# Order of the sparse-attention projections and index scores in a two-layer hybrid trunk

## The chip, the cores and the metric

One core of a Trainium2 chip runs the whole program in one launch. The metric is device time in microseconds (us): the median of repeated executions. TensorE is called PE here, VectorE DVE, ScalarE ACT, GpSimd POOL, SyncE SP, as in the profile's rows. L12 is line 12 of the kernel.

## The reference, cut to what matters

Two layers, 512 tokens of width 1024, float32. Each layer normalizes x and feeds one combined projection `w_in` into four branches: a gated convolution, a sparse attention with an indexer, a gated linear recurrence, and a cross-attention into 256 memory tokens. Each branch is lifted to width 1024, multiplied by its own sigmoid gate and summed; then an output projection with a residual, and a gated FFN with a residual.

The sparse attention is the part that the change touches. For each block of 128 queries:

```
rel    = relu(einsum('thd,sd->ths', iq, ik) * 64**-0.5)   # 8 index heads
score  = einsum('ths,th->ts', rel, iw);  future keys -> -inf
sel    = top 128 keys of score
p      = softmax(q @ k[sel] * 64**-0.5);  out = p @ v[sel]
```

The columns of `w_in` that feed it lie side by side: 512 for the queries, then 64 for the keys, 64 for the values and 512 + 64 + 8 for the index queries, the index keys and the index weights.

## The kernel before

Every big product is done as three matmuls of 32-bit parts: an operand is split into a high and a low part (hi, lo), and `mm3` (L318 to L328) adds hi*hi, hi*lo and lo*hi in PSUM (L324, L325, L327). Activations are kept split (`h_hi`, `h_lo`). A weight chunk (`Chunk`, L228) is loaded in parts of at most 1024 columns per partition by SP's DMA queue into `w_raw` (4 buffers); ACT copies the part to `w_hi` (L100) and DVE subtracts to get `w_lo` (L257), three buffers each, both at high priority. PE can use the part only after that. A chunk of 256 columns over all 1024 rows has two parts, one of 456 columns has four.

PSUM tiles come from three rotating groups: `mm` (3 banks), `at` (2) and `tr` (3).

A layer's mixer first runs four generators that each do a step and yield (L1033 to L1039). The order of their steps is a string of letters, `EARLY` (L45), one string for each layer:

- `b` is `projections` (L1008), three steps. Step one: the chunk of 256 columns (keys, values and the first two index heads), four token blocks of 24 matmuls each, evicted by `key_out` and worked up by `key_heads` (norm, rotation, transposes). Step two: the chunk of 456 columns (six index heads, the index key, the index weights), 96 matmuls for the four token blocks into three `mm` banks and one `tr` bank, evicted by `index_out`, worked up by `index_heads`. Step three: the queries, two chunks of 256 columns, 192 matmuls, then `query_heads`.
- `m` is `mem_branch` (L747), ten steps: a projection of two memory heads (48 matmuls of 512 columns), four steps of attention into the memory tokens (12 matmuls of 256 columns and four transposes each), and both once more.
- `c` is `conv_branch` (L715), six steps of 48 matmuls of 512 columns each.
- `s` is the selection: `select(1)`, `select(2)`, `select(3)` (L985) one after the other, five yields each. The first step of each is the scoring: for each of eight heads two matmuls ("dots", L841 and L842) into an `at` bank, a Relu on ACT into a scratch tile, and a multiply-add on DVE into `score` (L994, L996). `score` has one buffer, so a selection's scoring on DVE starts only when the one before is done. Four more steps hold four rounds each of MAX8 (L1002) and MATCH_REPLACE8 (L1003) on DVE, sixteen rounds in all, and a last operation writes the mask `bias` (L1006).
- `n` is the late norm, in the second layer only.

The scratch tile of the scoring is `wide()`, a group of four buffers, which `key_out`, `index_out` and the queries also use. Another group, `scratch512` (tile name `sq`, two buffers), holds squares of the norms and of the memory projection.

When the string is used up, `lift(3)` runs with six selection steps after each of its four steps (`weave`, L1039). Then `values` and `lift(0)` run woven with the attention blocks `attend(0)` to `attend(3)` (L844). An attention block needs `dots` of queries with keys, a masked maximum on DVE (L857), Exp on ACT, a reciprocal on DVE (L860), a scaling on ACT, and transposes of the probabilities on PE (L871). `attend(0)` needs no selection: its mask is the causal one. The first gate projection of `lift(0)` does its hi*hi and lo*hi products for all weights first and its products with `w_lo` at the end.

The letters and weaves give only a program order. A planner orders each engine's instructions when the program is built: it takes, on its own estimates of durations, the ready instruction of the highest priority, where earlier in the program means higher, and the weight splits and PSUM evictions are lifted above the rest. On the chip each engine then runs its list in that fixed order.

`after_two` and `after_los` (L226, L264 to L270) hold back named instructions until the next chunk's splits have been issued.

Of the kernel before, what the change touches and what calls it, by code (L numbers as in the profile page):

```python
# [25 lines left out]
KD = D // P  # L26
# [15 lines left out]
NONC = -2.0e38  # L42
OFF = -1.0e30
AHEAD = 3000
EARLY = ["mmbmcmcbmmmscsmcsssmccmbs", "mnmbmcmcbmmmscsmcsssmccmbs"]  # L45
MM_BUFS = 3
TR_BUFS = 3
AT_BUFS = 2
# [23 lines left out]
def hybrid_trunk(ctx: ExitStack, tc: tile.TileContext, x, mem, positions, norm_mix, w_in, conv_w,  # L72
# [33 lines left out]
    def mm_ps():  # L106
        return pmm.tile([P, 512], F32, name="mm")
# [4 lines left out]
    def tr_ps():  # L112
        return pat.tile([P, 512], F32, name="tr", bufs=TR_BUFS)
# [32 lines left out]
    ps = tr_ps()  # L146
# [16 lines left out]
    ps = tr_ps()  # L163
# [64 lines left out]
    class Chunk:  # L228
        def __init__(self, src, kt, n):
            self.kt, self.step = kt, min(kt, 1024 // n)  # L230
            self.parts = []
            for k in range(0, kt, self.step):
                e = min(kt, k + self.step)
                m = (e - k) * n
                raw, hi, lo = (wpool.tile([P, 1024], dt, name=nm, bufs=b)[:, :m].rearrange("p (k n) -> p k n", n=n)
                               for nm, dt, b in (("w_raw", F32, RAW_BUFS), ("w_hi", F32R, W_BUFS), ("w_lo", F32R, W_BUFS)))
                if len(src.shape) == 2:
                    loaded[0] = nc.sync.dma_start(raw, src[k * P:e * P].rearrange("(k p) n -> p k n", p=P))
                    raw_loads.append(loaded[0])
                    if len(raw_loads) == 2:  # L240
                        tc.add_manual_dep(mem_half.ins, loaded[0].ins.name, order, reason="weights first")
                    if keys:
                        tc.add_manual_dep(loaded[0].ins, keys.pop().ins.name, order, reason="keys first")
                else:
                    for g in range(2):
                        nc.sync.dma_start(raw.rearrange("p k (g c) -> p k g c", g=2)[:, :, g, :], src[:, k:e, g, :])
                with tc.high_priority(offset=AHEAD):
                    if len(raw_loads) == 1:
                        dve.tensor_copy(hi[:, 1:, :], raw[:, 1:, :])
                        i = A(hi[:, :1, :], raw[:, :1, :], AF.Copy)  # L250
                    else:
                        i = A(hi, raw, AF.Copy)
                    while len(self.parts) == 1 and before_second:
                        tc.add_manual_dep(i.ins, before_second.pop().ins.name, order, reason="probabilities first")
                    while behind:
                        tc.add_manual_dep(i.ins, behind.pop().ins.name, order, reason="accumulators first")
                    i2 = dve.tensor_sub(lo, raw, f(hi))  # L257
                    while low_after:
                        tc.add_manual_dep(low_after.pop().ins, i2.ins.name, order, reason="weights first")
                    while low_behind:  # L260
                        tc.add_manual_dep(i2.ins, low_behind.pop().ins.name, order, reason="operands first")
                    while after_hi:
                        tc.add_manual_dep(after_hi.pop().ins, i.ins.name, order, reason="weights first")
                    for a in after_two:  # L264
                        tc.add_manual_dep(a.ins, i.ins.name, order, reason="weights first")
                    for a in after_los:
                        tc.add_manual_dep(a.ins, i2.ins.name, order, reason="weights first")
                self.parts.append((range(k, e), hi, lo))
            after_two.clear()
            after_los.clear()  # L270
# [9 lines left out]
    def wchunk(src, kt, n):  # L280
        return Chunk(src, kt, n)
# [22 lines left out]
    def tokens_wide(ws, a, kt, pss, first=0, in_turn=False):  # L304

        k0, behind_part = 0, None
        for w in ws:
            for ks, _, _ in w.parts[0 if k0 else first:]:
                made = []
                for t, ps in enumerate(pss):  # L310
                    for k in ks:
                        made += mm3(ps, pair(a, k0 + k, slice(t * P, (t + 1) * P)), w.at(k), k0 + k == 0, k0 + k == kt - 1)
                for i in made if in_turn and behind_part is not None else []:
                    tc.add_manual_dep(i.ins, behind_part.ins.name, order, reason="part by part")
                behind_part = made[-1]
            k0 += w.kt
# [133 lines left out]
    h = new_h()  # L450
# [183 lines left out]
    def mixer(l, h, norms, cm):  # L634
# [197 lines left out]
        with pool_("dsa") as dp:  # L832
# [60 lines left out]
            with pool_("idx") as ip:  # L893
# [5 lines left out]
                def wide():  # L899
                    return ip.tile([P, S], F32, name="wide", bufs=4)  # L900
# [63 lines left out]
                def index_out(ps, t):  # L964
                    u = wide()
                    with tc.high_priority(offset=AHEAD):
                        A(u[:, :7 * HD], ps[:, :7 * HD], AF.Copy, scale=r_t[:, t:t + 1])
                        A(iw[:, t, :], ps[:, 7 * HD:7 * HD + 8], AF.Copy, scale=r8_t[:, t:t + 1])
                    return u

                def index_heads(u, t):
                    w = by_head(u)
                    rope(w[:, :7], 7, t)
                    dve.tensor_copy(w[:, 7, :], w[:, 6, :])
                    ps = turn_heads(u, 4)
                    twin_to(ikS, ps[:, 3 * P:], t)
                    heads_to(iqS, 2, ps[:, :3 * P], 6, t)
# [7 lines left out]
                def select(t):  # L985
                    n = (t + 1) * P
                    score = ip.tile([P, S], F32, name="score", bufs=1)[:, :n]
                    for hh in range(8):
                        ps = at_ps()[:, :n]
                        dots(ps, iqS, ikS, hh, t, n)  # L990
                        rel = wide()[:, :n]
                        A(rel, ps, AF.Relu, scale=HD ** -0.5)
                        if hh == 0:
                            dve.tensor_scalar(score, rel, iw[:, t, 0:1], 0.0, op0=OP.mult, op1=OP.add)  # L994
                        else:
                            dve.scalar_tensor_tensor(score, rel, iw[:, t, hh:hh + 1], score, op0=OP.mult,  # L996
                                                     op1=OP.add)
                    dve.copy_predicated(score[:, t * P:], future, neg.to_broadcast([P, P]))
                    yield
                    for i in range(TOPK // 8):  # L1000
                        m8 = ip.tile([P, 16], F32, name="m8", bufs=2)[:, :8]
                        dve.max(m8, score)  # L1002
                        dve.match_replace(score, m8, score, REPL)  # L1003
                        if i % 4 == 3:
                            yield
                    dve.tensor_scalar(biases[t], score, REPL, OFF, op0=OP.not_equal, op1=OP.mult)  # L1006

                def projections():  # L1008
                    w = wchunk(w_in[l][:, C_DK:C_DK + 256], KD, 256)
                    for t in range(NT):  # L1010
                        ps = mm_ps()[:, :256]
                        tokens(w, h, t, ps)
                        key_heads(key_out(ps, t), t)
                    yield
                    w = wchunk(w_in[l][:, C_DK + 256:C_DK + 712], KD, 456)
                    pss = [mm_ps()[:, :456] for _ in range(MM_BUFS)] + [tr_ps()[:, :456]]
                    tokens_wide([w], h, KD, pss, in_turn=True)
                    for t, u in enumerate([index_out(ps, t) for t, ps in enumerate(pss)]):
                        index_heads(u, t)
                    yield  # L1020
                    us = [wide() for _ in range(NT)]
                    for c in range(2):
                        w = wchunk(w_in[l][:, C_DQ + c * 256:C_DQ + (c + 1) * 256], KD, 256)
                        for t in range(NT):
                            ps = mm_ps()[:, :256]
                            tokens(w, h, t, ps)
                            with tc.high_priority(offset=AHEAD):
                                A(us[t][:, c * 256:(c + 1) * 256], ps, AF.Copy, scale=r_t[:, t:t + 1])
                            if c:
                                query_heads(us[t], t)  # L1030
                    yield
# [653 lines left out]
```

## Time and profile before

| quantity | value |
|---|---|
| median of 3 runs | 1975.92 us (1974.9 to 1976.09) |
| the profiled execution's own time | 1974.79 us |
| its span in the profile | 1972.8 us |
| mean granted TensorE clock | 0.998 of full speed |
| PE busy | 1958.9 us (99%) |
| DVE busy | 1466.6 us (74%) |
| ACT busy | 1169.3 us (59%) |

The span leaves out 1.99 us of the profiled execution that lie before and after the profile's first and last instruction. The profiled execution is 1.13 us below the median of the three runs. A "busy" PE includes waits that are hidden by the pipelined ends of matmuls, and a share of busy time is a mean over stages with different limits.

### The profile page before, as it was taken

To read this page: it belongs to the slowest core of one execution; us is meant where nothing else is said; L and a number is where in the kernel's file an instruction comes from. 1 tells how busy PE (TensorE), PEld (TensorE's weight loads), DVE (VectorE), ACT (ScalarE), POOL (GpSimd) and SP (SyncE) were. 2 spreads that over 40 slices of the span, in tenths; PEclk is the share of its full clock that TensorE was granted. 3 is DMA by queue.
4 is the path that set the end of the run, shared out by engine and by line. 5 is a ranking of instruction groups with operands and counts; after the bars stand their busy time and mean duration, and the time that the engine had idled before them with its cause. 6 is when DMAs were issued, how large, how long until landed. Compare 5 with 4: busy or idle time off the path is not lost.

```text
span 1972.8 us, 26656 instructions
## 1 busy us (share of the span) xinstructions
PE 1958.9 (99%) x9687; PEld 1636.0 (83%) x9687; DVE 1466.6 (74%) x2569; ACT 1169.3 (59%) x1958; POOL 236.2 (12%) x288
## 2 busy tenths in 40 slices
PE   9999999999999999999999999999999999999999
PEld 8888987878888888888888898878888888888887
DVE  7866998657876677786876699965678667867777
ACT  6754654766765456645654556477667655656564
POOL 1011111111111111100001111111111110111000
PEclk9999999999999999999999999999999999999999
DMA  8677666667687888886677767677777778898754
GB/s 304 207 179 168 172 160 166 161 139 172 166 210 186 231 232 255 244 245 188 202 218 168 181 144 174 148 182 157 167 177 162 209 198 251 250 266 235 213 186 139
DMA packets 222228, 385.25 MB, mean 195 GB/s; under 512 B 13194, under 2 KB 118224, under 8 KB 221840
## 3 DMA queue, kind: packets, MB, share of 16 engines
q1 hardware_dynamic: 163008, 244.16, 39.3%
q0 software_dynamic: 52192, 132.81, 33.3%
q10 hardware_dynamic: 6896, 6.58, 1.0%
q8 instruction: 76, 1.25, 0.3%
q14 instruction: 56, 0.46, 0.1%
HBM read 368.81 MB, written 140.51 MB: 258 GB/s over the span
## 4 chain that ended last, share of the span: by engine, by line
PE 97%; DVE 3%; ACT 0%; issue 0%; DVEq 0%; ACTq 0%
PE mm L327 24%; PE mm L324 23%; PE mm L325 23%; PE at L324 4%; PE at L325 4%; PE at L327 4%; PE tr L324 2%; PE tr L327 2%; PE tr L325 2%; PE tr L871 1%; PE tr L882 1%; PE tr L1577 1%; DVE score L1003 1%; PE at L842 1%; PE at L841 1%; DVE m L1002 1%
## 5 line engine op out<-in xcount | busy, mean ns | idle before, releaser
L100 ACT ACTIVATE w_hi<-w_raw 128x1024 fp32r<-128x1024 f32 (+1 forms) x435 | 457.3, 1054 | 353.1 <-PE mm L325 113.3
L324 PE MATMUL mm<-h_hi,w_hi 128*128 128x512 f32 x960 | 377.4, 394 | 0.6 <-DVE zg L1076 0.6
L325 PE MATMUL mm<-h_lo,w_hi 128*128 128x512 f32 x960 | 376.6, 392 | 0.0
L327 PE MATMUL mm<-h_hi,w_lo 128*128 128x512 f32 x960 | 374.8, 397 | 0.7 <-DVE w_lo L257 0.7
L1288 DVE TENSOR_TENSOR w_lo<-w_raw,w_hi 128x1024 fp32r<-128x1024 f32 x211 | 256.3, 1218 | 130.0 <-ACT w_hi L100 129.3
L257 DVE TENSOR_TENSOR w_lo<-w_raw,w_hi 128x1024 fp32r<-128x1024 f32 (+1 forms) x224 | 272.2, 1217 | 105.4 <-ACT w_hi L100 103.9
L1303 POOL DMA_DIRECT2D up_sums<-in_ffn_w_up_dram x120 | 121.5, 1012 | 836.5 <-DMA up_sums<-in_ffn_w_up_dram 554.6
L327 PEld LDWEIGHTS mm<-h_hi,w_lo 128*128 128x128 f32 x960 | 182.7, 190 | 37.6 <-DVE w_lo L257 0.8
L324 PEld LDWEIGHTS mm<-h_hi,w_hi 128*128 128x128 f32 x960 | 180.4, 188 | 36.3 <-issue 1.0
L325 PEld LDWEIGHTS mm<-h_lo,w_hi 128*128 128x128 f32 x960 | 180.4, 188 | 35.6 <-issue 0.2
L325 PE MATMUL mm<-w_lo,h_hi 128*128 128x512 f32 (+2 forms) x488 | 169.4, 347 | 0.3 <-DVE w_lo L257 0.3
L327 PE MATMUL mm<-w_hi,h_lo 128*128 128x512 f32 (+2 forms) x488 | 169.5, 347 | 0.0
L324 PE MATMUL mm<-w_hi,h_hi 128*128 128x512 f32 (+2 forms) x488 | 163.8, 347 | 0.0
L1303 POOL DMA_DIRECT2D w_sums<-in_ffn_w_down_dram x66 | 62.3, 944 | 331.8 <-DMA w_sums<-in_ffn_w_down_dram 186.2
L325 PEld LDWEIGHTS mm<-w_lo,h_hi 128*128 128x128 f32 x488 | 92.3, 189 | 11.3 <-DVE w_lo L257 0.6
L324 PEld LDWEIGHTS mm<-w_hi,h_hi 128*128 128x128 f32 x488 | 92.3, 189 | 10.5 <-ACT w_hi L100 0.2
L327 PEld LDWEIGHTS mm<-w_hi,h_lo 128*128 128x128 f32 x488 | 92.3, 189 | 10.2
L100 ACT ACTIVATE prob<-prob,small 128x128 f32<-128x128 f32 (+3 forms) x128 | 68.8, 554 | 33.6 <-DVE small L857 24.5
L327 PE MATMUL mm<-y_hi,w_lo 128*128 128x512 f32 x192 | 75.5, 393 | 0.0
L325 PE MATMUL mm<-y_lo,w_hi 128*128 128x512 f32 x192 | 75.4, 393 | 0.0
L324 PE MATMUL mm<-y_hi,w_hi 128*128 128x512 f32 x192 | 75.4, 393 | 0.0
L325 PE MATMUL mm<-w_lo,a_hi 128*128 128x512 f32 x160 | 63.2, 395 | 0.0
(496 smaller groups left out, 4191.6 us busy)
## 6 DMA issues: line engine op xcount, KB each, us to landing
w_raw<-in_w_in_dram SPq DMA_DIRECT2D x140, 512.0 KB, 4.6
up_sums<-in_ffn_w_up_dram POOLq DMA_DIRECT2D x120, 512.0 KB, 7.0
w_raw<-up_sums SPq DMA_DIRECT2D x80, 512.0 KB, 5.3
w_raw<-in_ffn_w_up_dram SPq DMA_DIRECT2D x60, 512.0 KB, 4.6
w_sums<-in_ffn_w_down_dram POOLq DMA_DIRECT2D x54, 512.0 KB, 6.1
up_sums<-up_sums POOLq DMA_DIRECT2D x40, 512.0 KB, 5.1
w_raw<-in_w_lift_dram SPq DMA_DIRECT2D x32, 512.0 KB, 4.6
w_raw<-in_ffn_w_down_dram SPq DMA_DIRECT2D x24, 512.0 KB, 5.0
```

Of the source, the lines that this page charges most:

```text
L100: i = act.activation(dst, src, func, **kw)
L257: i2 = dve.tensor_sub(lo, raw, f(hi))
L324: made += [pe.matmul(ps, ah, bh, start=first, stop=False, skip_group_check=more), pe.matmul(ps, ah, bl, start=False, stop=False, skip_grou ...
L325: pe.matmul(ps, ah, bl, start=False, stop=False, skip_group_check=more)]
L327: made += [pe.matmul(ps, al, bh, start=False, stop=last, skip_group_check=more)]
L841: return [pe.matmul(ps, q[:, hh, s], k[0][:, :n], start=True, stop=False), pe.matmul(ps, q[:, hh, s], k[1][:, :n], start=False, stop=True)]
L842: pe.matmul(ps, q[:, hh, s], k[1][:, :n], start=False, stop=True)]
L871: turn = pe.transpose(pp[:, (2 * e + i) * P:(2 * e + i + 1) * P], probs[2 * i + e][:, b * P:(b + 1) * P], ident)
L882: i = pe.matmul(pv[e * HD:(e + 1) * HD, c], vt[:, b, :], pt[:, b, e * 2 * P:(e + 1) * 2 * P], start=b == 0, stop=b == t)
L1002: dve.max(m8, score)
L1288: two = A(hi, raw, AF.Copy), dve.tensor_sub(lo, raw, f(hi))
L1303: i = nc.gpsimd.dma_start(dst, src, **kw)
```

## The change

The three steps of `projections` are put in another order: the chunk of 456 index columns first, then the chunk of 256 key columns, then the queries. The two `EARLY` strings are changed so that the index chunk stands behind one memory step (in the second layer behind the late norm too), the key chunk behind two more memory steps, the scoring of `select(1)` behind six memory steps and one convolution step in place of seven and two, and the scoring of `select(2)` ahead of the queries in place of behind them. Each letter occurs as often as before. The Relu of the scoring writes a `scratch512` tile in place of a `wide` tile. In `Chunk`, the instructions held in `after_two` and `after_los` wait for the first two parts of a chunk, not for all of them.

```diff
-EARLY = ["mmbmcmcbmmmscsmcsssmccmbs", "mnmbmcmcbmmmscsmcsssmccmbs"]
+EARLY = ["mbmmbcmmmsccsmmcsssmsccmb", "mnbmmbcmmmsccsmmcsssmsccmb"]
...
-                    for a in after_two:
+                    for a in after_two if len(self.parts) < 2 else []:
                         tc.add_manual_dep(a.ins, i.ins.name, order, reason="weights first")
-                    for a in after_los:
+                    for a in after_los if len(self.parts) < 2 else []:
                         tc.add_manual_dep(a.ins, i2.ins.name, order, reason="weights first")
...
                     for hh in range(8):
                         ps = at_ps()[:, :n]
                         dots(ps, iqS, ikS, hh, t, n)
-                        rel = wide()[:, :n]
+                        rel = scratch512(n)
                         A(rel, ps, AF.Relu, scale=HD ** -0.5)
...
                 def projections():
+                    w = wchunk(w_in[l][:, C_DK + 256:C_DK + 712], KD, 456)
+                    pss = [mm_ps()[:, :456] for _ in range(MM_BUFS)] + [tr_ps()[:, :456]]
+                    tokens_wide([w], h, KD, pss, in_turn=True)
+                    for t, u in enumerate([index_out(ps, t) for t, ps in enumerate(pss)]):
+                        index_heads(u, t)
+                    yield
                     w = wchunk(w_in[l][:, C_DK:C_DK + 256], KD, 256)
                     for t in range(NT):
                         ps = mm_ps()[:, :256]
                         tokens(w, h, t, ps)
                         key_heads(key_out(ps, t), t)
-                    yield
-                    w = wchunk(w_in[l][:, C_DK + 256:C_DK + 712], KD, 456)
-                    pss = [mm_ps()[:, :456] for _ in range(MM_BUFS)] + [tr_ps()[:, :456]]
-                    tokens_wide([w], h, KD, pss, in_turn=True)
-                    for t, u in enumerate([index_out(ps, t) for t, ps in enumerate(pss)]):
-                        index_heads(u, t)
                     yield
                     us = [wide() for _ in range(NT)]
```

## Rows read from the trace of the kernel before

**Rows 1.** The page's first part: busy us of each engine, share, instructions.

```profile
PE 1958.9 (99%) x9687; PEld 1636.0 (83%) x9687; DVE 1466.6 (74%) x2569; ACT 1169.3 (59%) x1958; POOL 236.2 (12%) x288
```

**Rows 2.** Waits of PE: who waited for whom, total us, times, longest us.

```profile
PE tr L871 <- ACT prob L100: 5.7, 2, 3.5
...
PE mm L327 <- DVE w_lo L257: 0.7, 1, 0.7
```

**Rows 3.** The chain of waits, first layer: start us, us, what.

```profile
309.88 0.67 DVE score L1003 x2
...
328.12 3.41 DVE w_lo L257 x3
332.42 5.25 PE mm L327 x16
```

**Rows 4.** Timeline of PE, first layer: start, us, instruction, idle before.

```profile
320.28 0.22 PE L841 MATMUL at<-k_hi,qS 128*128 128x128 f32 x1
...
321.19 0.39 PE L324 MATMUL mm<-h_hi,w_hi 128*128 128x512 f32 x1
...
327.77 0.39 PE L325 MATMUL mm<-h_lo,w_hi 128*128 128x512 f32 x1
...
328.35 0.28 PE L842 MATMUL at<-k_lo,qS 128*128 128x128 f32 x1
332.09 0.33 PE L871 MATMUL tr<-ident,prob 128*128 128x128 f32 x1 [3.46 <-ACT prob L100]
332.17 5.50 PE L327 MATMUL mm<-h_hi,w_lo 128*128 128x512 f32 x16
337.51 0.39 PE L324 MATMUL mm<-y_hi,w_hi 128*128 128x512 f32 x1
```

**Rows 5.** Timeline of DVE in the same stretch.

```profile
327.27 0.43 DVE L1006 TENSOR_SCALAR bias<-score 128x512 f32<-128x512 f32 x1
327.62 0.29 DVE L857 CUSTOM_DVE_ANT_0 prob<-at,causal_bias 128x128 f32<-128x128 f32 x1
...
328.04 3.49 DVE L257 TENSOR_TENSOR w_lo<-w_raw,w_hi 128x1024 fp32r<-128x1024 f32 x3
331.45 0.22 DVE L860 RECIPROCAL small<-small 128x1 f32<-128x1 f32 x2
```

**Rows 6.** Timeline of PE at the same place of the second layer.

```profile
1285.17 0.50 PE L327 MATMUL mm<-h_hi,w_lo 128*128 128x512 f32 x1 [0.69 <-DVE w_lo L257]
1287.95 0.33 PE L871 MATMUL tr<-ident,prob 128*128 128x128 f32 x1 [2.28 <-ACT prob L100]
1288.03 5.27 PE L327 MATMUL mm<-h_hi,w_lo 128*128 128x512 f32 x15
1293.13 0.39 PE L324 MATMUL mm<-y_hi,w_hi 128*128 128x512 f32 x1
```

**Rows 7.** Windows: busy us PE, PEld, DVE, ACT, POOL; clock; DMA.

```profile
150.00:183.00 33.00, 33.00 (x161) 27.67 (x161) 17.09 (x33) 12.00 (x25) 4.88 (x6) 1.00 0.69 174
183.00:328.00 145.00, 145.00 (x771) 125.33 (x769) 136.22 (x294) 74.91 (x133) 22.43 (x26) 1.00 0.67 158
...
332.20:337.60 5.40, 5.40 (x18) 4.30 (x19) 2.19 (x4) 3.60 (x10) 0.00 (x0) 0.68 0.95 294
```

**Rows 8.** Timeline of PE: the first dots of the first scoring.

```profile
168.55 0.28 PE L841 MATMUL at<-ik_hi,iqS 128*128 128x256 f32 x1
```

**Rows 9.** Timeline of DVE: first MAX8 of the layer; first head of the third scoring.

```profile
192.54 0.42 DVE L1002 MAX8 m<-score 128x8 f32<-128x256 f32 x1
...
287.83 0.49 DVE L994 TENSOR_SCALAR score<-wide,iw 128x512 f32<-128x512 f32 x1
```

**Rows 10.** Timeline of ACT: Relus of the third scoring, around its start on DVE.

```profile
259.26 1.09 ACT L100 ACTIVATE wide<-at 128x512 f32<-128x512 f32 x2
265.00 0.57 ACT L100 ACTIVATE wide<-at 128x512 f32<-128x512 f32 x1
...
289.49 1.06 ACT L100 ACTIVATE wide<-at 128x512 f32<-128x512 f32 x2
```

**Rows 11.** DMA issues: the 456-column parts, count, KB each, us to landing.

```profile
w_raw<-in_w_in_dram SPq DMA_DIRECT2D x8, 456.0 KB, 4.2
```

## The prediction

> **What bounds the kernel now.** I read the page's busy times first: PE is busy 1958.9 us of 1972.8 [rows 1], so only 13.9 us are idle, and everything that a change of order can win lies there or in work at a low clock. The waits of PE come next: of what they name, the largest by far are two waits for a probability, 5.7 us together, and a neighbour for a `w_lo`, 0.7 us [rows 2]. The chain of waits shows where: just ahead of that place in each layer the chain leaves PE and runs along DVE, from round to round of the third selection, then through three `w_lo` splits, and back to PE [rows 3]. The two timelines show how. PE has its first dots of `attend(0)` done at 320.6 us; DVE is in the rounds until the mask is written at 327.27 us and turns to the attention's maximum at 327.62 us, 7 us late; three `w_lo` of 3.49 us stand behind it; the reciprocal comes at 331.45 us and the transposed probability at 332.09 us, after 3.46 us of idle PE [rows 4, 5]. The second layer shows the same with idle times of 0.69 and 2.28 us [rows 6]. So at this place, and there alone, DVE sets the end; elsewhere PE does.
>
> After each wait PE also runs slow. A 512-column matmul starts every (327.77 - 321.19) / 29 = 0.227 us before it, and the 16 matmuls behind it take 337.51 - 332.17 = 5.34 us, 0.334 each [rows 4]; the granted clock of that stretch is 0.68 [rows 7], a mean of time at 1.2 and at 2.4 GHz after an engine that idled.
>
> **What the place costs.** First layer: 3.46 us idle, and 5.34 - 16 x 0.227 = 1.71 us of slow matmuls. Second: 0.69 + 2.28 = 2.97 us, and 15 matmuls in 1293.13 - 1288.03 = 5.10 us, less 15 x 0.227 = 3.40, gives 1.70 us [rows 6]. Sum: 5.17 + 4.67 = 9.84 us. That is what the change can win.
>
> **The change part by part.**
>
> *Index chunk ahead, scoring earlier.* PE's work is the same in number and shape; it changes place. Ahead of the first scoring now stand six memory steps in place of seven and one convolution step in place of two. A convolution step is 48 matmuls of 0.227 us, 10.9 us. The memory step has 12 matmuls and four transposes, none longer than 0.227 us, so between 0 and 3.6 us; I take 2. The first dots, at 168.55 us [rows 8], come about 12.9 us earlier, and the first MAX8, at 192.54 us [rows 9], with them.
>
> What that is worth is read from DVE. Between 183 and 328 us it is busy 136.2 of 145 us, so it is full: the selections, the queries' norms and the gates all queue there. Between 150 and 183 us it is busy 17.1 of 33, 48% idle [rows 7]. DVE's total work is unchanged, and rounds of MAX8 need nothing but DVE, so each microsecond by which the selections start earlier fills idle DVE time at that rate: 12.9 x 0.48 = 6.2 us by which the third selection ends earlier. Bounds: 0, if the planner puts other DVE work there, and 12.9, if all the time gained were idle before. I take 6.2. The probability would be ready at 332.09 - 6.2 = 325.9 us, and PE has other work until 328.6 us [rows 4]; so the wait goes with 2.7 us to spare, and the slow matmuls with it. In the second layer 2.97 us have to go, with a little more to spare. What is late next there is `w_lo`: its three splits also move forward with the queue, so I see none.
>
> *Second scoring ahead of the queries.* It cannot start on DVE before the first selection's last round, since `score` has one buffer. It lets the second selection's rounds mix with the queries' DVE work and not stand behind it. DVE is full in that stretch, so this reorders and gains nothing by itself; what it costs is that the queries are done later, and their cover is 65 us and more of `lift(3)` ahead of the first use (4 x 72 matmuls of 0.227). I cost it at 0. Without that cover, a late query would bring a wait like the one removed, 5.17 us.
>
> *Scratch of two buffers.* The change adds a wait: the Relu of head h now waits until DVE has multiplied head h - 2; before it was h - 4. Behind the waiting Relu on ACT stand the next weight splits and the gates' sigmoids; PE waits for `w_hi`. Before, Relus of the third scoring run at 259.26 and 265.00 us, over 20 us ahead of DVE's first head at 287.83 us, and two more at 289.49 us as soon as two buffers are free [rows 9, 10]. Such a lead is lost for two heads. Two ends: 0, if ACT's order has the Relu that late anyway and half of ACT is idle, 75 of 145 us busy [rows 7]; and 5.17 us, one whole stall of the size seen, for each layer. Nearest is the row in which ACT already takes its Relus in this manner without any wait of PE; I take 0.5 us for each layer, mostly of DVE.
>
> *Shared tiles.* The `sq` tiles hold the memory projection's squares just before the first scoring, so its first two Relus wait for PE's column sums, which lie ahead of the dots in PE's own order: 0. The keys now take the four `wide` tiles right behind the index heads, with two memory steps between: the keys' eviction can wait for the index heads' rotations. Ends: 0, and one wait of PE of 3.46 us for each layer. I take 0, as the first key block needs 24 matmuls before it is evicted.
>
> *Loads.* The four parts of the index chunk, 456 KB each, landing in 4.2 us [rows 11], now stand in SP's queue ahead of the keys' two parts and of the first memory values, and their four ACT and four DVE splits ahead as well. PE takes 24 matmuls of 456 columns for a part, at most 24 x 0.227 = 5.4 us and about 5, so queue, ACT and DVE keep pace: 0; ends 0 and one landing, 4.2 us. POOL's queue is not passed. The limit to two parts keeps the held instructions as they were, since only the 456-column chunk has more: 0.
>
> **The sum.** -9.84 + 2 x 0.5 = -8.8 us. The profiled execution took 1974.79 us, so 1966.0 us; the median of the runs is 1.13 us above it, so 1967.1 us. I forecast 1967 us. With the stalls gone in full and nothing new it is 1966.1.
>
> **Rivals.**
>
> *Half a gain.* DVE gains 2 to 3 us, not 6: the earlier selection work lands on DVE slots that convolution evictions fill anyway. For it: just before 183 us the idle time is partly made of waits for ACT and PE, and the moved convolution step brings its own DVE work behind the scoring. Against: DVE is half idle there over 33 us. Then the waits shrink by 2.5 us in each layer and the slow matmuls stay: 1975.9 - 5 = 1971 us.
>
> *No change.* The planner moves the dots of `attend(0)` and the transposes by as much as the selections, since it orders by its own estimates and DVE is later on the chip than planned; the distance of 7 us between PE's dots and DVE's turn stays. For it: PE's order already has only 7.8 us of work between the dots and the transpose. Against: the dots' place follows from PE's work, which is the same. 1974 to 1978 us.
>
> *Slower: two buffers tie three engines together.* Place: the second and third scoring, where DVE is full. A Relu waits on a late DVE, ACT's weight split stands behind it, and PE runs out of split weights. It decides from the point at which DVE is later than planned by more than PE's stock of two parts, 2 x 24 x 0.227 = 10.9 us; the lateness seen is 7 us, so it needs half as much again. If it comes once in each layer and the old waits stay, it costs another 2 x 4.92 us: 1985.7 us. The Trainium skill speaks for it: in Perfetto Trace Analysis, Optimization Strategy, it says that the same gap repeating on the engine that should be saturated can mean too few buffers for the next tile. By that rule fewer buffers should bring gaps at each scoring; the trace before shows no wait of PE for an `at` bank or for ACT in the scorings, with four.
>
> **How the numbers follow.** Forecast 1965 to 1969.5 us: 0.52. Half a gain: 0.18. No change: 0.17. Slower: 0.13. About 0.2% (4 us) is what a measurement of this kernel can tell from no change, so faster is below 1972.0 and slower above 1979.9. Of half a gain 0.12 falls below 1972: faster 0.64, same 0.23, slower 0.13. Low end: all idle time named by the waits and the slow matmuls gone, with a microsecond of scatter, 1963.5. High end: no change with its scatter, 1977.5; beyond it lie the slower case and a rest.
>
> **What would show it.** The selection's last mask should be written near 321 us in the first layer in place of 327.27, and as much earlier in the second; the waits for a probability should be gone from PE's list, and the granted clock be full behind the first transposes. The first dots should stand near 156 us, and DVE be fuller between 150 and 183 us. The half gain shows as shorter waits at the same place; no change as the mask and the first attention dots moving together; the slower case as Relus that wait for DVE's `score` and PE waiting for `w_hi` behind them. Wrong altogether: PE idle anew in the projections, waiting for `wide` tiles or the index chunk's parts.

## The result, and the profile after

The changed kernel takes 1989.5 us (median of 4 runs) against 1976.0 for the kernel before in the same comparison: ratio 1.007, interval 1.0052 to 1.0087. It is 13.5 us slower, where 1967 was forecast. Its profiled span is 1987.5 us.

The page's busy times and the waits of PE (columns as in [rows 1, 2]), kernel after:

```profile
PE 1961.3 (99%) x9687; PEld 1637.2 (82%) x9687; DVE 1463.7 (74%) x2569; ACT 1170.0 (59%) x1958; POOL 235.8 (12%) x288
```

```profile
PE tr L871 <- ACT prob L100: 9.3, 2, 6.3
PE at L841 <- DVE small L857: 6.9, 1, 6.9
PE mm L324 <- DVE merged L682: 1.6, 2, 1.2
PE at L324 <- ACT mpt_hi L100: 1.4, 2, 0.7
...
PE mm L543 <- ACT w_hi L100: 0.7, 1, 0.7
```

PE has the same 9687 matmuls. Idle time is 1987.5 - 1961.3 = 26.2 us against 13.9 [rows 1], and busy time is 2.4 us more, at a mean granted clock of 0.995 against 0.998; together the 14.7 us of the spans. The waits that were to go are longer: 16.2 us at L871 and L841 against 5.7 at L871 [rows 2]. No new wait for `w_hi` stands in the list.

The timeline of PE at the place of [rows 4] (first two lines) and of [rows 6] (the rest):

```profile
322.80 0.27 PE L842 MATMUL at<-k_lo,qS 128*128 128x128 f32 x1
336.44 0.48 PE L871 MATMUL tr<-ident,prob 128*128 128x128 f32 x1 [6.28 <-ACT prob L100]
...
1297.99 0.48 PE L841 MATMUL at<-k_hi,qS 128*128 128x128 f32 x1 [6.92 <-DVE small L857]
1302.12 0.48 PE L871 MATMUL tr<-ident,prob 128*128 128x128 f32 x1 [3.01 <-ACT prob L100]
```

And DVE there, for [rows 5]:

```profile
331.62 0.43 DVE L1006 TENSOR_SCALAR bias<-score 128x512 f32<-128x512 f32 x1
331.96 0.28 DVE L857 CUSTOM_DVE_ANT_0 prob<-at,causal_bias 128x128 f32<-128x128 f32 x1
...
332.38 3.49 DVE L257 TENSOR_TENSOR w_lo<-w_raw,w_hi 128x1024 fp32r<-128x1024 f32 x3
335.79 0.22 DVE L860 RECIPROCAL small<-small 128x1 f32<-128x1 f32 x2
```

It is the old place, only later: the third mask is written at 331.62 us, 4.35 later than in [rows 5] and 10.6 later than forecast, and the same three splits stand behind it. The second layer loses more (PE's waits there are 9.93 us against 2.97).

Yet the selection began early. First dots and first MAX8, for [rows 8, 9]:

```profile
150.92 0.28 PE L841 MATMUL at<-ik_hi,iqS 128*128 128x256 f32 x1
...
175.52 0.43 DVE L1002 MAX8 m<-score 128x8 f32<-128x256 f32 x1
```

They are 17.6 and 17.0 us earlier. So the lead was lost between 175 and 331 us. Windows of busy time tell where (columns as in [rows 7]); first the kernel after:

```profile
150.00:183.00 33.00, 33.00 (x162) 27.73 (x161) 23.58 (x53) 12.12 (x25) 5.06 (x6) 1.00 0.75 175
...
200.00:240.00 40.00, 40.00 (x274) 37.51 (x274) 25.14 (x55) 19.69 (x38) 5.73 (x7) 1.00 0.70 165
240.00:280.00 40.00, 38.15 (x178) 31.23 (x177) 39.74 (x94) 24.65 (x48) 6.62 (x8) 1.00 0.71 161
...
1156.00:1196.00 40.00, 40.00 (x286) 38.03 (x285) 25.35 (x57) 19.39 (x39) 5.48 (x8) 1.00 0.66 148
```

(the last line is the place of the second layer), and the kernel before in the second and third of these:

```profile
200.00:240.00 40.00, 40.00 (x282) 37.56 (x282) 36.58 (x99) 23.67 (x54) 5.54 (x6) 1.00 0.69 178
240.00:280.00 40.00, 40.00 (x184) 33.32 (x183) 37.99 (x74) 23.19 (x37) 6.62 (x9) 1.00 0.64 142
```

DVE won 23.58 - 17.09 = 6.5 us up to 183 us [rows 7], and lost 36.58 - 25.14 = 11.4 us from 200 to 240. PE is fully busy in both, so PE's waits show nothing of it there. PE idles 1.85 us in the next window, where it was full before; most of the bill comes 100 us later. DVE's timeline of the window from 200 us says what it lacked:

```profile
208.57 0.29 DVE L1006 TENSOR_SCALAR bias<-score 128x256 f32<-128x256 f32 x1
...
215.96 0.42 DVE L994 TENSOR_SCALAR score<-sq,iw 128x384 f32<-128x384 f32 x1 [2.25 <-ACT sq L100]
...
221.67 0.62 DVE L996 SCALAR_TENSOR_TENSOR score<-sq,iw,score 128x384 f32<-128x384 f32 x1 [1.75 <-ACT sq L100]
...
234.53 0.36 DVE L998 COPY_PREDICATED_SCALAR score<-future,neg 128x128 f32 x1
...
236.90 0.69 DVE L794 TENSOR_REDUCE small<-at 128x2 f32<-128x512 f32 x1 [0.17 <-PE at L327]
...
240.90 0.68 DVE L921 TENSOR_REDUCE small<-hn_sq 128x8 f32<-128x512 f32 x1
```

The first selection ends at 208.57 us; the second cannot start until the second scoring is through, at 234.53, and that scoring keeps DVE waiting. The work that could fill part of the time, the norms of the queries' heads (L921 first), comes only at 240.90, behind the first reduction of the last memory step (L794, here called m10, the last `m` of the order string). Before, it came at 217.33:

```profile
217.33 0.69 DVE L921 TENSOR_REDUCE small<-hn_sq 128x8 f32<-128x512 f32 x1
```

ACT's timeline, kernel after, shows that the norm could have run then: its input `hn_sq` is written from 216.33 us on. It also shows what spreads the scoring: the first Relu waits 3.09 us for PE's dots, which PE runs from 214.9 to 231.1 us among the queries' matmuls.

```profile
215.44 0.49 ACT L100 ACTIVATE sq<-at 128x384 f32<-128x384 f32 x1 [3.09 <-PE at L842]
...
216.33 0.63 ACT L100 ACTIVATE hn_sq<-wide 128x512 f32<-128x512 f32 x1
```

### The profile page after: what moved, and what is told of

Same layout as the page of the kernel before. It is cut to its first block, busy times and chain, and to the rows that moved or that the text cites. A ratio compares the mean times of both kernels' runs of the same rounds, so it can differ in the third digit from the quotient of the medians.

```text
span 1987.5 us, 26679 instructions
## 1 busy us (share of the span) xinstructions
PE 1961.3 (99%) x9687; PEld 1637.2 (82%) x9687; DVE 1463.7 (74%) x2569; ACT 1170.0 (59%) x1958; POOL 235.8 (12%) x288
## 3 DMA queue, kind: packets, MB, share of 16 engines
q8 instruction: 76, 1.25, 0.3%
## 4 chain that ended last, share of the span: by engine, by line
PE 94%; DVE 5%; issue 0%; ACT 0%; DVEq 0%; ACTq 0%
PE mm L327 23%; PE mm L324 23%; PE mm L325 23%; PE at L324 4%; PE at L327 4%; PE at L325 4%; DVE score L1003 2%; PE tr L324 2%; PE tr L325 1%; PE tr L327 1%; DVE m L1002 1%; PE tr L871 1%; PE tr L882 1%; PE tr L1577 1%; PE at L842 1%; PE at L841 1%
## 5 line engine op out<-in xcount | busy, mean ns | idle before, releaser
L100 ACT ACTIVATE w_hi<-w_raw 128x1024 fp32r<-128x1024 f32 (+2 forms) x435 | 457.5, 1054 | 343.5 <-PE mm L325 113.3
L324 PEld LDWEIGHTS mm<-w_hi,h_hi 128*128 128x128 f32 x488 | 92.3, 189 | 10.5 <-ACT w_hi L100 0.2
```

What stands on the lines that cost most here:

```text
L100: i = act.activation(dst, src, func, **kw)
L324: made += [pe.matmul(ps, ah, bh, start=first, stop=False, skip_group_check=more), pe.matmul(ps, ah, bl, start=False, stop=False, skip_grou ...
```

## The experiments

Each median stands beside runs of the kernel before in its own comparison (1974.6 to 1976.0 us); ratios are to those. In an order string the last `b` is the queries, the sixth `s` begins the second scoring, and the second layer has the same string with an `n` behind its first letter.

**Two buffers or four, and the second scoring's place.** The first three undo one part each.

```diff
 # e1, in select()
-                        rel = scratch512(n)
+                        rel = wide()[:, :n]
 # e2, first layer
-EARLY = ["mbmmbcmmmsccsmmcsssmsccmb", ...
+EARLY = ["mbmmbcmmmsccsmmcsssmccmbs", ...
```

e4 is e2 with the line of e1; e3 is the kernel before with `scratch512(n)` in place of `wide()`.

> The changed kernel with one thing undone: the Relu writes the group of four buffers again. Theory Q (the second scoring and its rounds stand ahead of the queries' work in DVE's fixed list, the scoring waits for PE's dots, and DVE sits idle some 15 us of 40 behind the first selection): the idle DVE time stays, only what the third scoring grew by (1.2 and 2.4 us) goes, so 1984 to 1988 us. Rival B (the two buffers pace the scorings and so make all three selections late): back to 1976 us or below.

> The changed kernel with only the letter of the second scoring moved back behind the queries; index chunk first and two buffers stay. Theory Q: DVE's idle time behind the first selection goes, the earlier start of the first selection is kept, the mask of the third selection comes 4 to 6 us earlier than in the kernel before, and the time is 1967 to 1973 us. Rival B: the two buffers still pace the scorings, 1984 to 1990 us.

> The kernel before with one thing changed: the Relu writes the group of two buffers. Theory Q: only the third scoring grows, by 1 to 2.5 us in each layer, and the mask comes that much later: 1977 to 1981 us. Rival B: 1985 to 1990 us.

> Index chunk first, first scoring earlier, but the second scoring behind the queries and four buffers: the part of the change that was to win time, by itself. Theory Q: 1965 to 1971 us, with the waits for a probability gone or under 1 us. Rival B says the same. A third theory, that the order of the chunks itself costs: above 1976 us.

Measured: e1 1975.83 us (1.0001, 0.9992 to 1.0011); e2 1981.48 (1.0033, 1.0021 to 1.0045); e3 1977.47 (1.0010, 1.0000 to 1.0019); e4 1977.63 (1.0013, 1.0004 to 1.0023). So two buffers cost 13.7 us with the second scoring ahead (after less e1), 3.9 with it behind (e2 less e4), 2.4 in the old order (e3 less its before, 1975.0 us; its interval reaches down to no loss). The second scoring ahead costs 8.0 us with two buffers (after less e2) and gains 1.8 with four (e1 less e4). And the index chunk first, with neither, is worth nothing (e4): its first mask comes at 208.78 us, 12.6 earlier than before, but the second selection then waits for a scoring that starts on DVE at 232.12 (233.12 before), and the third mask comes at 326.02, only 1.25 earlier. So theory Q held for e3 alone; e1 came out as rival B, e4 as the third theory, and e2 between the two that were named for it.

e1 has the earlier mask that was forecast, 319.24 us, and no wait at L871, and still gains nothing. Its third mask, the largest of its waits of PE, and its windows of both layers:

```profile
319.24 0.43 DVE L1006 TENSOR_SCALAR bias<-score 128x512 f32<-128x512 f32 x1
```

```profile
PE tr L808 <- DVE mprob L806: 2.9, 2, 2.6
```

```profile
200.00:240.00 40.00, 37.77 (x262) 34.15 (x261) 35.84 (x89) 20.52 (x48) 6.71 (x7) 1.00 0.64 153
...
1156.00:1196.00 40.00, 36.08 (x236) 32.38 (x236) 33.19 (x84) 20.25 (x44) 6.70 (x9) 0.91 0.51 122
```

DVE has most of its work back, and now PE runs dry: 2.2 and 3.9 us idle, with a granted clock of 0.91 in the second window. In this stretch and order, DVE is fed and PE starves with four `wide` buffers; with two scratch buffers it is the other way round.

**What the place is worth.** The kernel before with 11 of the 16 rounds of the third selection; it leaves out 5 rounds of MAX8 and replacement.

> The kernel before with 11 rounds in place of 16 in the third selection (that part of the selection is left out), which takes 5 x 1.52 = 7.6 us from DVE ahead of the first attention block. If the place costs what the prediction says, the waits for a probability and the slow matmuls behind them go and the time falls by 8 to 10 us, to 1965 to 1968 us. If PE has another wait right behind, less than 5 us.

Measured: 1964.57 us (0.9947, 0.9932 to 0.9962), clock 1.0, no wait at L871. The place costs about 10 us (10.5 by the ratio, 10.0 by the medians), as worked out (9.84).

**Priority.** e5 raises the queries' head norms by half of `AHEAD`; e13 puts m10 ahead of the second scoring (`...sssmmsccb`) and raises all scoring by `AHEAD`.

> The changed kernel with the queries' norms, rotations and transposes at a raised priority, so that the planner puts them on DVE before the second scoring is through. If the loss is DVE's idle time of 15 us behind the first selection, with the queries' work waiting in the list behind the rounds, that time is filled, the third mask comes near 320 us and the kernel takes 1966 to 1976 us. If two buffers alone pace the scorings whatever stands beside them: 1984 us or more.

> Two buffers, m10 ahead of the second scoring, and all scoring raised in the plan's priority. If the third scoring's length is what is left of the loss, its first-to-last accumulation falls back to about 13 us in the first layer, the waits at L871 and L841 together fall from 12 to 6 to 9 us, the time from 1981 to 1976 to 1979. If it is readiness and not priority, nothing moves: 1980 to 1982.

Measured: 1989.95 us (1.0076, 1.0059 to 1.0092), L921 still at 241.08 us; 1980.92 (1.0031, 1.0019 to 1.0043), which is its twin without the raise (e9, below). A raised priority moved nothing in either; for e5 I had forecast 1966 to 1976 us. What held the norms in the plan these runs do not show: on the chip their input was there at 217 us.

**Holding the queries.** e7 holds the queries' matmuls behind the last dots of the second scoring; e8 is e1 with a convolution step between (`...sssmcscmb` for `...sssmsccmb`).

```diff
 # e7, in projections()
-                            tokens(w, h, t, ps)
+                            for i in tokens(w, h, t, ps):
+                                tc.add_manual_dep(i.ins, scored[-1].ins.name, order, ...)
```

> The changed kernel, two buffers kept, with the queries' matmuls held in PE's order behind the last dots of the second scoring, as the shared tiles of the kernel with four buffers hold them. Theory H (with a scratch of its own the scoring loses that hold, the planner mixes query products into it and DVE waits for dots): the second scoring takes under 10 us on DVE and the time is 1974 to 1979 us. Theory N (two buffers by their number): the scoring still takes 15 us or more and the time is 1984 us or more.

> The version with four buffers, and the second scoring behind one of the two convolution steps that stood behind it, so that PE has 10.9 us of work between the memory step and the scoring. In the version with four buffers the mask of the third selection came 8 us early and no probability was waited for, but PE waited near 205 to 215 and 1160 to 1170 us for the memory step's probabilities and the scoring. If these waits ate the gain, they go: 1965 to 1971 us. If the gain went elsewhere: 1974 us or more.

Measured: e7 1988.5 us (1.0067, 1.0052 to 1.0082). DVE's timeline of its second scoring, in which L996 and L998 are the old L994 and L996:

```profile
208.69 0.42 DVE L996 TENSOR_SCALAR score<-sq,iw 128x384 f32<-128x384 f32 x1
...
211.06 4.23 DVE L998 SCALAR_TENSOR_TENSOR score<-sq,iw,score 128x384 f32<-128x384 f32 x6 [0.79 <-ACT sq L100]
```

The second scoring is prompt with two buffers (its heads on DVE from 208.7 to 215.3 us), the third mask comes at 315.82, the wait at L871 is gone, but PE waits 9.1 us for the memory probabilities. Theory H is right on the scoring and 9.5 us or more off on the time. Two buffers by their number do not make the scoring slow; PE's planned order does, in which the queries' matmuls stand between the dots. e8 1975.87 (1.0004, 0.9995 to 1.0014), e1 in all but name: the convolution step did not fill PE's idle time.

**m10's place and the number of buffers.**

```diff
 # e9
-EARLY = ["mbmmbcmmmsccsmmcsssmsccmb", ...
+EARLY = ["mbmmbcmmmsccsmmcsssmmsccb", ...
 # e10: the third of three is the tile of the queries' squares
+                        rel = scratch512(n) if hh % 3 < 2 else ip.tile([P, S], F32, name="hn_sq", bufs=1)[:, :n]
 # e11
+                        rel = scratch512(n) if hh % 2 else wide()[:, :n]
```

e12 is e9 with the line of e1.

> The changed kernel with its two scratch buffers, but the memory step m10 stands ahead of the second scoring, not behind it. Theory M (VectorE stands idle for some 15 us of 200 to 240 because the norms of the queries' heads come in its order only behind m10's first reduction, and m10 stands behind a scoring that two buffers make slow): the first norm reduction of the queries (L921) comes before the second scoring ends, VectorE is busy at least 32 of the 40 us from 200 to 240 where the changed kernel has 25.1, the third mask of the first layer comes at 322 to 328 and not at 331.6, the waits for the first probability (L871) fall to 4 to 12 us from 17.6, and the time is 1974 to 1981. Rival R (the slow scoring alone delays the second and with it the third selection, whatever else VectorE finds to do): third mask at 330 to 333, time 1986 to 1991.

> The changed kernel, each third Relu into the buffer of the queries' squares, so three buffers in all. If the number of buffers sets how long the second scoring takes (18.6 us on VectorE with two, 7.1 with four), it takes 8 to 13 us here, m10's first reduction comes at 220 to 230 and not at 236.9, the third mask at 322 to 328, the time at 1976 to 1983. If two buffers cost only by being shared with something else, three do as two did: scoring 17 to 20 us, 1986 to 1991.

> The changed kernel, every second Relu into a wide buffer, the others into the norms' two: six buffers in all, the queries' tiles held up by half as many Relus as with the wide buffers alone. Theory M and the reading of the wide-buffer run (third mask 8 us earlier, its gain given back because TensorE runs out of work while the queries' evictions stand behind the scoring): the second scoring takes 7 to 10 us, the third mask comes at 318 to 324, no wait at L871 over 1 us, and TensorE loses less at 200 to 220 than there: 1967 to 1975. If TensorE is stalled by VectorE's lateness with the memory probabilities and not by the queries' tiles, it loses the same and the time is 1975 to 1977.

> The kernel with wide buffers (four), with the memory step m10 ahead of the second scoring. Theory M: with a prompt scoring the place of m10 matters little to VectorE, third mask 319 to 323; the memory probabilities are asked for earlier, before the eight scored rows, so TensorE's waits for them (L808, 2.9 us and a second at low clock) shrink: 1969 to 1975. If m10 ahead only moves TensorE's idle time, 1975 to 1978.

Measured: e9 1981.05 us (1.0029, 1.0017 to 1.0041). Its windows:

```profile
200.00:240.00 40.00, 40.00 (x281) 37.59 (x280) 32.21 (x80) 24.18 (x55) 5.48 (x6) 1.00 0.64 165
...
1156.00:1196.00 40.00, 40.00 (x278) 37.33 (x278) 29.74 (x71) 22.60 (x51) 6.72 (x9) 1.00 0.60 157
```

DVE has 7.1 us of its work back in the first layer and 4.4 in the second, the queries' first norm is at 217.1 us, the first layer's mask at 327.82, and 8.5 us of the time return. That is theory M, at the edge of its time; R fell. e10 1987.14 (1.0059, 1.0044 to 1.0074): a third buffer changes little (2.4 us; the second scoring's heads from 216 to 233 us), but this one is also the tile of the queries' squares, so the run does not test the number alone. e11 1975.7 (1.0004, 0.9994 to 1.0013): half the Relus in `wide` do what all do (third mask 318.88 us); my reading that PE's loss would halve is wrong. e12 1985.34 (1.0052, 1.0037 to 1.0066), a miss: with four buffers m10 ahead is worse by 9.5 us than behind the scoring, PE waiting 7.4 us for memory probabilities.

**m10 behind the queries.**

```diff
 # e14; e15 is e14 with the line of e1
-EARLY = ["mbmmbcmmmsccsmmcsssmsccmb", ...
+EARLY = ["mbmmbcmmmsccsmmcsssmsccbm", ...
 # e16, with the line of e1
+EARLY = ["mbmmbcmmmsccsmmcsssscmbcm", ...
```

> Two buffers, m10 behind the queries, at the end of the early steps. Theory M (VectorE starves because the queries' norms stand behind m10 in its order): the first norm comes at 212 to 220, VectorE is busy 30 to 36 of the 40 us from 200 to 240, the third mask of the first layer comes at 321 to 328, the time is 1972 to 1981. Rival R (the scoring, slow in two buffers, holds back the second selection whatever stands behind it): third mask at 330 to 333, 1986 to 1991.

> Four wide buffers, m10 behind the queries. If TensorE's idle time at 207 to 216 comes from m10 in front of the queries, it shrinks from 2.2 us to under 1 us per layer, the third mask stays at 317 to 321, and the time is 1967 to 1973. If it comes from the queries' tiles standing behind the scoring's, TensorE idles as before or more there: 1975 to 1982.

> Four wide buffers, second scoring right behind the first selection, then a conv step, m9, the queries, the last conv step, m10. If TensorE only lacks work that is ready at 207 to 216 in the run with wide buffers, the conv step's products fill it: under 1 us idle per layer, third mask 317 to 322, 1967 to 1973. If what is moved ahead is missing later, TensorE idles elsewhere by as much: 1975 to 1980.

Measured: e14 1973.17 us (0.9992, 0.9983 to 1.0001). Two letters exchanged give back all that the change had lost, 16.3 us. DVE's timeline of e14 and its windows:

```profile
216.75 0.69 DVE L921 TENSOR_REDUCE small<-hn_sq 128x8 f32<-128x512 f32 x1 [0.61 <-ACT hn_sq L100]
...
234.43 0.61 DVE L996 SCALAR_TENSOR_TENSOR score<-sq,iw,score 128x384 f32<-128x384 f32 x1
...
237.95 0.69 DVE L794 TENSOR_REDUCE small<-at 128x2 f32<-128x512 f32 x1
```

```profile
200.00:240.00 40.00, 40.00 (x277) 37.56 (x277) 32.31 (x79) 23.05 (x52) 6.50 (x7) 1.00 0.66 166
...
1156.00:1196.00 40.00, 40.00 (x272) 37.22 (x271) 33.10 (x78) 23.64 (x52) 6.72 (x9) 1.00 0.59 153
```

The second scoring is as slow as in the kernel after, its last head at 234.43 us, and m10's reduction as late, 237.95. Only the norms have come out from behind m10, to 216.75, and they give DVE 7.2 us of the 11.4 back. The slow scoring alone is not the loss; the empty time around it is. e9 fills the first layer as well as e14 does, but not the second: there DVE has 25.35 us in the kernel after, 29.74 in e9 and 33.10 in e14, and PE's waits at L871 and L841 are 9.9, 8.2 and 1.7 us. That is most of the 7.9 us between e9 and e14.

e15, the same order with four `wide` buffers, takes 1986.47 us (1.0058, 1.0041 to 1.0075); e16 1985.46 (1.0053, 1.0038 to 1.0068). Both lie beyond every time that I had named for them. Their third masks are early (321.50 and 319.32 us), and the time is lost on PE. Waits and window of e15:

```profile
PE mm L324 <- DVE gate L665: 5.8, 4, 2.1
PE tr L808 <- DVE mprob L806: 2.9, 2, 2.6
```

```profile
240.00:280.00 40.00, 36.83 (x163) 29.13 (x162) 37.81 (x80) 25.59 (x45) 6.45 (x8) 0.96 0.69 161
```

So m10's move is worth -16.3 us with two buffers and +10.6 with four (e15 less e1): neither part has a price of its own.

**What two buffers still cost, and both memory steps behind.**

```diff
 # e17, on e14
-                        rel = scratch512(n)
+                        rel = wide()[:, :n] if t == 3 else scratch512(n)
 # e18, on e17
+EARLY = ["mbmmbcmmmsccsmmcssssccbmm", ...
```

> m10 behind the queries, two scratch buffers for the first and second scoring, four wide ones for the third. If two buffers still cost the third scoring 1 to 2.4 us per layer, its first-to-last accumulation in the first layer falls from 13.3 to 12 us or less, the waits at L871 fall from 3.6 to 0 to 2 us, and the time is 1969 to 1972.5. If the third mask is early enough already, the wait only moves: 1972.5 to 1975.

> Both memory steps m9 and m10 behind the queries, the second scoring right behind the first selection, two scratch buffers, the third scoring in wide ones. If the memory steps between them make the scoring slow, its accumulations take 7 to 11 us instead of 15, the third mask comes at 315 to 321, no wait at L871, and the time is 1965 to 1972. If the two buffers make it slow, 14 to 19 us and 1972 to 1978. If the memory steps are late for what follows them (the wait for the gates at L665 seen with m10 behind and wide buffers), 1975 to 1987.

Measured: e17 1967.09 us (0.9957, 0.9944 to 0.9971), faster than both kernels: 8.5 us less than before, 22.4 less than after. The page's busy times of e17, its DVE timeline, and its window:

```profile
PE 1955.6 (100%) x9687; PEld 1633.9 (83%) x9687; DVE 1463.8 (74%) x2569; ACT 1169.1 (59%) x1958; POOL 235.9 (12%) x288
```

```profile
324.33 0.43 DVE L1006 TENSOR_SCALAR bias<-score 128x512 f32<-128x512 f32 x1
...
1276.00 0.43 DVE L1006 TENSOR_SCALAR bias<-score 128x512 f32<-128x512 f32 x1
```

```profile
200.00:240.00 40.00, 40.00 (x277) 37.57 (x277) 32.31 (x79) 23.04 (x52) 6.70 (x7) 1.00 0.68 166
```

PE's idle time is 1964.9 - 1955.6 = 9.3 us, no wait at L871 or L841 is left, and the mean clock is 1.0. It is also below both of the times that I had named. Only the third scoring's buffers tell e17 from e14: two in place of four cost 6.1 us, and its last head starts at 297.0 us in e14, at 292.0 in e17.

e18 1983.82 us (1.0043, 1.0031 to 1.0056). The group of the second scoring's second to eighth heads (count, ns min/median/max, first and last start):

```profile
L996 DVE SCALAR_TENSOR_TENSOR score<-sq,iw,score x7: 609/618/621, 208.4 to 217.7; 128x384 f32<-128x384 f32 x7
```

The same group in e17:

```profile
L996 DVE SCALAR_TENSOR_TENSOR score<-sq,iw,score x7: 610/614/620, 219.1 to 234.4; 128x384 f32<-128x384 f32 x7
```

And the window of e18:

```profile
240.00:280.00 40.00, 32.04 (x141) 25.78 (x140) 36.81 (x81) 23.01 (x41) 6.45 (x8) 0.87 0.64 141
```

The two buffers take 9.3 us here, against 15.3 in e17; four take 5.2 in e1 (211.6 to 216.8). So part of the spread came from the memory steps that stood around the scoring. But PE then idles 8 us of 40; its waits name the memory probabilities (L806, 4.9 us) and the gates (L665, 4.7 us). Quick second scorings (4.8 to 4.9 us in e12 and e15) stand in slow kernels, and a slow one, 15.3 us, in the fastest.

## Why the prediction was wrong

Forecast was -8.8 us, measured +13.5. Step by step: the index chunk first alone gives +2.6 us (e4) in place of -9.84; the second scoring ahead, with four buffers, -1.8 (e1 less e4) in place of 0; the two buffers on top of both +13.7 (after less e1) in place of 1.0. That makes 14.5; the kernel before differs by 1.0 us between the two comparisons.

- **The place and its price: right.** 9.84 us by the rows; 10.0 to 10.5 by e6, and 8.5 of them taken by e17.
- **Index chunk ahead: right up to the first mask, wrong from there on.** Forecast 6.2 us of DVE time, measured 6.5 up to 183 us. The first mask came 12.8 us earlier (12.9 forecast for the first dots, which came 17.6 earlier). The step that failed is "by which the third selection ends earlier": in e4, which has this part without the two others, the third mask comes 1.25 us earlier, and none of the 9.84 us are won. The lead ends at the second scoring, which stands behind the queries; with that scoring ahead and prompt the lead reaches the third mask (8.0 us in e1), and there PE loses near the memory steps what it wins.
- **Second scoring ahead of the queries, costed at 0: the step that made the loss, together with the next.** It said "DVE is full in that stretch, so this reorders and gains nothing by itself". With four buffers 0 is nearly right (e1 less e4, -1.8 us); with two it costs 8.0 us (after less e2). [Rows 7] show DVE full in an order in which the queries' norms run beside the end of the first selection. The change puts the second scoring and m10 ahead of the norms in DVE's planned order; DVE stood idle for 14.9 of 40 us, 11.4 more than before, while the norms' input was ready from 217 us on. e14 shows it by moving m10 alone. The cover that I named, the 65 us of `lift(3)` for late queries, was there; the late queries were harmful as missing filling for DVE, not as late results.
- **Scratch of two buffers, 0.5 us per layer: mis-sized.** In the order of the change it is 13.7 us (e1), 6.8 a layer and beyond the upper bound of 5.17. In the third scoring alone it is 6.1 us in e17's order, 3.05 a layer: six times the value taken. In the first two scorings it is a gain with m10 behind: e17 beats e15 by 19.4 us. With the Relus in `wide` the queries' first norm comes at 225 us (e1, e11, e15), in scratch at 217 (e14, e17); that the Relus hold the `wide` tiles that the queries need is my reading of it, which no run tests alone. I asked whom fewer buffers would delay, not whom the freed ones would let go. And I added up parts that have no price apart from each other.
- **Shared tiles and loads: right.** The 456 KB parts landed in 6.8 us in place of 4.2 [rows 11], and no wait of PE names a load there or a `wide` tile.
- **The rivals.** Slower came true, and the two buffers that it named are half of the cause (e1), but by another path: PE's waits for `w_hi` stayed at 0.7 us, and DVE ran empty in place of late. The rule of the Trainium skill cited there (Perfetto Trace Analysis, Optimization Strategy) looks for the gap on the engine that should be saturated; here PE has none in the second scoring (40.00 of 40 us busy), the gap is on DVE, and PE pays at 330 us. No change and half a gain fell.

Open is which resource orders the norms behind m10 in the plan. Both draw on the one ring of 12 `small` tiles, and m10 and the dots share the `at` banks; separate tiles were not tried. Open too is why the plan in e10 spreads three buffers as it does two. No run undoes the limit to two parts in `Chunk` by itself; it is in the kernel after and in every run on it, and its price of 0 stays untested.

## What to carry to other kernels

A stretch in which an off-path engine is full is full in that order only: before moving work, list what would be next on that engine if the moved part is slow, and check that something ready stands behind it. Taking one user out of a shared scratch ring changes the order of the others, and that can be worth more than the number of buffers (here 19.4 us one way, 6.1 the other, in one kernel). Try the order string and the buffers together: here neither gave a gain alone (e14 and e1).

## What the runs showed that was not expected

Idle time has two prices, by engine. DVE's 14.9 idle us at 200 to 240 cost PE nothing there; PE has lost 5.4 us by its first L882 (at 362.36 us, at 357.00 before), part of it at 240 to 280 us and the rest behind 330. PE's idle time is paid at once. Where it was long the granted clock fell with it (the 1.85 us at 240 to 280 left it at 1.00): 0.87 in e18's window with 8 us idle, and 0.82, a mean of time at 1.2 and at 2.4 GHz, where PE starts again behind the wait of 6.28 us in the kernel after:

```profile
336.40:348.00 11.60, 11.56 (x49) 9.66 (x50) 6.45 (x19) 8.22 (x21) 2.36 (x2) 0.82 1.00 258
```
